# More column products by seven, folded norm factors, and values copied to blocks in DRAM: one encoder layer on one core

## The chip, the cores and the metric

The kernel runs on one core of a Trainium2 chip. Times are device microseconds. The time before is a median of 1103.4 us of three runs (1100.61 to 1104.03). The profile shows one further execution, with a span of 1101.0 us and a time of 1102.79 us. Engines are TensorE (PE, with its weight loads as PEld), VectorE (DVE), ScalarE (ACT), GpSimd (POOL) and SyncE (SP); SP issues nearly all DMAs, in order.

## The reference

One layer, 2048 tokens of width 1024, 16 heads of 64, all float32. The token grid is 32 rows by 64 columns.

```python
h = rmsnorm(x, g)                            # h = x * rsqrt(mean(x^2) + 1e-6) * g
q, k, v, gate = split(h @ w_in, 4)           # w_in is 1024 x 4096
# neighbourhood attention: a query at (row, col) sees 8 rows x 16 columns of keys,
# s = q.k / 8 + bias(head, row offset, col offset), softmax, o = p @ v
x = x + (o * silu(gate)) @ w_out
out = rmsnorm(x, norm_f)
```

## The kernel before, in words

Precision: every matrix operand is split into a high part rounded to fp32r and a low part, and each product is three matmuls, high by high, high by low and low by high. A matmul moves 512 columns.

The tokens are four column blocks c of 512, c = 0 to 3 (8 grid rows each). A *unit* is 256 output columns of q, k or the gate g; `(kind, j)` with j = 0 to 3 names them, and one unit holds two head pairs hp = 2j and 2j + 1. Values v are made in two units u, token tile t by token tile (t = 0 to 15).

**Stage one** (`stage_one`) makes v for tiles 0 to 7 and all 12 units of k, q, g for the token blocks 0 and 1. The units go by `seven_products`: the product of a 2 x 2 block matrix (two halves of the input width by two halves of the unit's columns, against two token blocks) is formed from seven block products in place of eight, in the order 1, 6, 2, 7, 5, 4, 3. One block product is 12 matmuls (4 k-tiles by 3), so a unit is 84. Its inputs are token blocks B11, B12, B21, B22 (first index: half of the input width, second: token block) and sums T1 to T4 of them, made once; and weight quarters A11 to A22 with sums S1 to S4, made for each unit on DVE (`sum_`). Each is split by `form` (ACT, then DVE), up to six products ahead. After the products, `keep`, `add` and `out_` combine the PSUM banks into the four outputs. `out_` adds on DVE and multiplies by `rb[c]` on GpSimd; `evac` does the fourth output with one DVE multiply. `rb[c]` is the reciprocal root mean square of the 512 tokens of block c, spread over the partitions: `diagonal(c)` puts it on four diagonal matrices, `spread_rstd(c)` multiplies by ones (two matmuls) and copies the bank (ACT). The gain g is put in when the x blocks are split (`split_to` with a scale). `give` then finishes an output: k into a high and a low part, g to g(1 + tanh(g/2)), q as it is; and it queues the store to DRAM (`k_hi`, `k_lo`, `sgd`, `qd`).

**Stage two** (`stage_two`) makes v for tiles 8 to 15 and the units of `units_two`, three of them (k, q, g with j = 0), by seven products for the token blocks 2 and 3. `evac_v` scales by the reciprocal root mean square of the token (`rt`).

**Attention** is a loop of 64 pairs, plus two to drain. A step is one head pair p and one row block T (8 query rows, up to 15 key rows); a *pair* is half of a step, two of the four column groups C. `order` has T = 0 for all p first, then T = 1 and 2, then T = 3. Iteration i does, in this order on each engine: `begin(i)` (mask additions `bias` on GpSimd, and loads asked for), `feed` (other TensorE work), `middle(i)` (split of the queries), `feed` again, `normalise(i-1)` (reciprocal on DVE, multiply on GpSimd), `turns(i-2)` (transposes of the probabilities, copied out of PSUM by DVE, L1011, and ACT, L1010), `scores(i)` (L963; mask and minimum on DVE, L970; exponential on ACT, L973), `values(i-2)` (L1031, and after a step's second pair the product with the gate, L1045).

`feed(n)` takes n matmuls from a generator, so that TensorE has work while the other engines do the softmax. Its second call has `calm` 8: it goes on, up to 12 matmuls, until 8 have passed since the last item given to DVE and ACT. `amount[i]` is 22 matmuls for the first 48 pairs and 19.7 for the last 18. The fill is first `projections`: the columns of k, q, g with j = 1 to 3 for token blocks 2 and 3, in `halves`, two groups of 24 matmuls each (`group`, lines L365, L367, L369), evacuated at once by `evac` (`pending`, `flush`). Then `outputs`: the output projection, tile by tile (L1223 to L1227), with `split_og` (L1103, L1104) of the loaded attention output, residual, and final norm. What is left of it runs alone after the loop.

Loads and stores are closures in the list `later` with a due time in matmuls of fill; `due` issues them on SP. `must` issues a store early if a load needs it. Tiles come from pools with a fixed number of buffers, each freed when its last reader is done; a DMA into a buffer still in use waits on SP, and with it all DMAs behind it. The value cache `vd` has the layout [head pair, grid row mod 4, column, row group, 128]; `load_v` (L920) reads a block for a column group by four DMAs, one for each row within a group of four. A program lists the functions that the diff touches:

## Time and profile before

| | |
|---|---|
| median of three runs | 1103.4 us (1100.61 to 1104.03) |
| profiled execution | 1102.79 us, span 1101.0 us |
| TensorE busy | 1080.7 us, 98% |
| DVE, ACT, POOL busy | 732.7, 531.5, 378.5 us |
| DMA traffic | 217.29 MB, mean 197 GB/s |
| granted TensorE clock, mean | 0.99 |

A row of the table of stretches is: start and end; duration; busy time of PE, PEld, DVE, ACT and POOL, each with its number of instructions; granted clock; busy share of the DMA engines; GB/s. A row of a group has busy time and mean ns of one, then the idle time of the engine before them with what ended it. In a timeline row the bracket is the idle time before the first instruction of the row and its releaser. In the chain of waits a row is start, length, and what ran.

### The profile page before, as it was taken

The numbers are of one execution on the slowest core, as the hardware profiler recorded it, in microseconds if no ns is written. First come the engines' busy times: TensorE is split into PE (matmuls) and PEld (weight loads), VectorE is DVE, ScalarE is ACT, GpSimd is POOL, SyncE is SP. The second block draws the span as 40 slices with busy tenths as digits, with TensorE's granted clock in tenths as the row PEclk, the third lists the DMA queues.
The fourth block names the chain that finished last, engine by engine and source line by source line (L and its number), as shares of the span: only waits on it lengthen the run. The fifth ranks groups of instructions, "written<-read, shape, count | busy, mean of one in ns | idle before, by whom it ended". The sixth has DMA issues, their size and how long they took to land.

```text
span 1101.0 us, 22543 instructions
## 1 busy us (share of the span) xinstructions
PE 1080.7 (98%) x7657; PEld 883.6 (80%) x7657; DVE 732.7 (67%) x1663; ACT 531.5 (48%) x1336; POOL 378.5 (34%) x483
## 2 busy tenths in 40 slices
PE   9999999999999999999999999999999999999997
PEld 6888888888888888877888888888877888887885
DVE  5376778788777337575665766665777777776644
ACT  7545343343344433255554554564556555555422
POOL 0000312222130001245445444424447666675200
PEclk9999999999999999998999999999999999999999
DMA  8633545454574235587767878687979797887452
GB/s 307 209 96 105 185 132 181 143 173 112 166 216 138 80 89 157 195 263 232 233 193 241 251 223 230 211 268 222 259 237 286 228 288 225 252 274 211 152 153 77
DMA packets 142962, 217.29 MB, mean 197 GB/s; under 512 B 18048, under 2 KB 65408, under 8 KB 142848
## 3 DMA queue, kind: packets, MB, share of 16 engines
q1 hardware_dynamic: 142704, 215.58, 64.6%
q8 instruction: 62, 1.02, 0.4%
q14 instruction: 52, 0.43, 0.1%
q10 hardware_dynamic: 144, 0.26, 0.1%
HBM read 157.05 MB, written 58.72 MB: 196 GB/s over the span
## 4 chain that ended last, share of the span: by engine, by line
PE 88%; DVE 5%; DMA 3%; issue 2%; ACT 1%; POOL 1%; SPq 0%; DVEq 0%; POOLq 0%
PE pp L421 24%; PE pv L534 16%; PE o L1031 7%; PE s L963 6%; PE pp L369 6%; PE pp L367 6%; PE pp L365 5%; PE po L1227 5%; PE po L1223 4%; PE po L1225 4%; PE ph L986 4%; ACT x L973 1%; PE zp L1242 1%; DVE gl L1104 1%; DMA sgt<-sgd 0%
## 5 line engine op out<-in xcount | busy, mean ns | idle before, releaser
L981 POOL TENSOR_SCALAR x<-x,st 128x360 f32<-128x360 f32 (+5 forms) x256 | 143.1, 579 | 239.1 <-DVE st L979 157.1
L439 POOL TENSOR_TENSOR tmp<-tmp,rb 128x512 f32<-128x512 f32 x45 | 73.5, 1634 | 399.2 <-DVE tmp L438 358.4
L973 ACT ACTIVATE x<-x,st 128x360 f32<-128x360 f32 (+5 forms) x256 | 151.8, 594 | 56.4 <-DVE st L970 56.4
L421 PE MATMUL pp<-h,f 128*128 128x512 f32 x480 | 155.4, 389 | 0.0
L945 POOL TENSOR_TENSOR em<-e,mk 128x480 f32<-128x480 f32 (+5 forms) x160 | 140.8, 915 | 5.0 <-DVE st L970 5.0
L421 PE MATMUL pp<-t,f 128*128 128x512 f32 x540 | 129.8, 389 | 0.1
L970 DVE CUSTOM_DVE_ANT_0 x<-s,em 128x360 f32<-128x360 f32 (+5 forms) x256 | 123.8, 538 | 5.1 <-PE s L963 2.0
L421 PEld LDWEIGHTS pp<-t,f 128*128 128x128 f32 x540 | 101.3, 188 | 21.5 <-DVE u L432 0.6
L369 PE MATMUL pp<-h,w 128*128 128x512 f32 x288 | 115.9, 403 | 0.0
L367 PE MATMUL pp<-l,w 128*128 128x512 f32 x288 | 114.2, 397 | 0.0
L365 PE MATMUL pp<-h,w 128*128 128x512 f32 x288 | 113.6, 394 | 0.0
L1010 ACT ACTIVATE pta<-ph 96x256 f32<-96x256 f32 (+1 forms) x224 | 58.8, 333 | 105.8 <-PE ph L986 105.8
L1031 PEld LDWEIGHTS o<-pta,vt 96*64 96x64 f32 (+2 forms) x1792 | 86.0, 139 | 24.2 <-DVE pta L1011 10.2
L421 PEld LDWEIGHTS pp<-h,f 128*128 128x128 f32 x480 | 90.1, 188 | 18.8
L1031 PE MATMUL o<-pta,vt 96*64 96x128 f32 (+4 forms) x1792 | 95.2, 258 | 7.5 <-DVE pta L1011 4.6
L1227 PE MATMUL po<-wol,gh 128*128 128x512 f32 x252 | 101.4, 403 | 0.0
L1223 PE MATMUL po<-woh,gh 128*128 128x512 f32 x252 | 100.0, 397 | 0.0
L1225 PE MATMUL po<-woh,gl 128*128 128x512 f32 x252 | 99.7, 395 | 0.0
L1011 DVE COPY pta<-ph 128x384 f32<-128x384 f32 (+3 forms) x128 | 60.5, 513 | 51.5 <-PE ph L986 51.2
L421 PE MATMUL pp<-l,f 128*128 128x512 f32 x240 | 93.4, 389 | 0.0
L534 PE MATMUL pv<-wh,h 128*128 128x512 f32 x256 | 88.1, 390 | 0.0
L534 PE MATMUL pv<-wh,l 128*128 128x512 f32 x256 | 88.0, 389 | 0.0
(136 smaller groups left out, 1951.1 us busy)
## 6 DMA issues: line engine op xcount, KB each, us to landing
raw<-in_wg_dram SPq DMA_DIRECT2D x126, 256.0 KB
e<-in_rpb_dram SPq DMA_DIRECT2D x54, 240.0 KB
vt<-vd SPq DMA_DIRECT2D x256, 48.0 KB
row<-in_xr_dram SPq DMA_DIRECT2D x32, 256.0 KB
vd<-v SPq DMA_DIRECT2D x32, 256.0 KB
k_hi<-hi SPq DMA_DIRECT2D x32, 256.0 KB
k_lo<-lo SPq DMA_DIRECT2D x32, 256.0 KB
qd<-tmp SPq DMA_DIRECT2D x32, 256.0 KB
```

The costliest lines, as they stand in the source:

```text
L365: nc.tensor.matmul(p, wh[w, b][:, cols], hh[k, c], start=(k == 0), stop=False)
L367: nc.tensor.matmul(p, wh[w, b][:, cols], hl[k, c], start=False, stop=False)
L369: nc.tensor.matmul(p, wl[w, b][:, cols], hh[k, c], start=False, stop=(k == NK - 1))
L421: nc.tensor.matmul(B[n, P], t[:, int(m == 2), c], x[k][int(m == 1)], start=P in (1, 6, 5) and k == 0 and m == 0, stop=k == 3 and m == 2, s ...
L534: nc.tensor.matmul(ps[t], a[:, o], b, start=k == 0 and m == 0, stop=k == NK - 1 and m == 2)
L945: (nc.gpsimd if attending[0] or not s else nc.vector).tensor_tensor(sh(t), E[p, s][:, u0 + 4:u1 + 4, v0 + 8:v1 + 8], sh(MK[0][:, m0:m0 + n ...
L973: nc.scalar.activation(X[i, C][s], X[i, C][s], AF.Exp, bias=st[:, s:s + 1], scale=-1.0, accum_out=st[:, 2 + s:3 + s])
L981: nc.gpsimd.tensor_scalar(X[i, C][s], X[i, C][s], st[:, 4 + s:5 + s], 0.5, op0=OP.mult, op1=OP.mult)
L1031: nc.tensor.matmul(o[s * 64:s * 64 + 64, C * 128 + q0:C * 128 + q0 + nq], vt[C][:k, g - g0_, s * 64:s * 64 + 64], t[:k, at:at + nq], start ...
L1223: nc.tensor.matmul(p, gh, woh[q, j], start=(i == 0), stop=False)
L1225: nc.tensor.matmul(p, gl, woh[q, j], start=False, stop=False)
L1227: nc.tensor.matmul(p, gh, wol[q, j], start=False, stop=(i == NK - 1))
```

## The change

Six units are made by seven products in stage two (j = 0 and 1) in place of three; `halves` keeps j = 2 and 3, and `amount` follows by its formula: 16 matmuls for each of the first 48 pairs.

For the token blocks 2 and 3 the gain and the reciprocal root mean square go into the input blocks: `normed` multiplies a block of x by both in place on DVE, before it is split or summed. The outputs of stage two and of `projections` are then not scaled: `give` reads the bank itself. `diagonal(2)`, `spread_rstd(2)` and `diagonal(3)` move into the last units of stage one, `spread_rstd(3)` to the first value tiles of stage two. The gate is no longer kept in the column-blocked order; the product with the attention output reorders it.

Values are copied from `vd` to `vc[p, C]`, one DRAM tile for each head pair and column group, in two halves of rows (`copy_v`): 32 copies in stage one's products (three to a unit), 32 in the last value tiles and the products of stage two. `load_v` then needs one DMA for a block.

Queries are loaded two steps ahead into a pool of one buffer (`lp`) and split one step ahead, in the second pair of a step. The due times of the loads of values, keys, bias rows and gate change. `quiet` is a flag that lets `split_og` go two turns ahead in the second pair of a step, and late otherwise.

```diff
+    vc = {(p, C): dram.tile([4 * (c1 - c0), 8, 128], F32, name=f"vc{p}_{C}")
+          for p in range(NP) for C, (c0, c1) in enumerate(KEY_COLS)}
...
         if kind == "x":
-            split_x(a, b, t, (hh[a, b], hl[a, b]))
+            normed("x%d1" % (a // 4 + 1), b, a % 4, t)
+            split_to(hh[a, b], hl[a, b], t, None)
...
-    units_two = [(k, j) for j in range(1) for k in "kqg"]
-    halves = [(k, j, 1, c) for j in range(1, 4) for g in (("k", "q", "g") if j < 3 else ("k", "qg")) for c in (2, 3) for k in g]
+    units_two = [(k, j) for j in range(2) for k in "kqg"]
+    halves = [(k, j, 1, c) for j in range(2, 4) for g in (("k", "q", "g") if j == 2 else ("k", "qg")) for c in (2, 3) for k in g]
...
-    def give(kind, hp, c, tmp):
+    def give(kind, hp, c, t, psum=False):
...
         if kind == "q":
-            store(("q", hp, c), 12, lambda: nc.sync.dma_start(qd[hp][:, s], tmp))
+            if psum:
+                o = ev([128, 512], F32, "q")
+                nc.scalar.activation(blocked(o), tiled(t), AF.Copy)
+                t = o
+            store(("q", hp, c), 12, lambda: nc.sync.dma_start(qd[hp][:, s], t))
...
-        nc.scalar.activation(v, p, AF.Copy, scale=rt[:, t:t + 1])
+        nc.scalar.activation(v, p, AF.Copy, scale=rt[:, t:t + 1] if t < 8 else 1.0)
...
             nc.vector.tensor_tensor(lay(tmp), of(B[n, P]), of(u), OP.add)
-            nc.gpsimd.tensor_tensor(lay(tmp), lay(tmp), of(rb[c]), OP.mult)
+            if c0 == 0:
+                nc.gpsimd.tensor_tensor(lay(tmp), lay(tmp), of(rb[c]), OP.mult)
...
+    def normed(f, c, k, t):
+        nc.vector.scalar_tensor_tensor(t, t, gain(f, k), rb[c], op0=OP.mult, op1=OP.mult)
...
+    def copies(h, n):
+        for _ in range(n):
+            if uncopied[h]:
+                copy_v(*uncopied[h].pop(0))
...
         def also(n, i):
             m = n + len(us) - 1
+            if m and i in (1, 3, 5):
+                copies(0, 1)
...
+            if (n, i) == (-3, 1):
+                diagonal(2)
+            if (n, i) == (-3, 3):
+                spread_rstd(2)
...
+        norms = {(-2, 3): ("x11", 0), (-2, 5): ("x11", 1), (-1, 0): ("x11", 2), (-1, 1): ("x11", 3),
+                 (-1, 3): ("x21", 0), (-1, 4): ("x21", 1), (-1, 5): ("x21", 2), (-1, 6): ("x21", 3)}
...
         def also(n, i):
+            copies(1, 1)
...
-        def rows(r):
-            if r == 0:
-                VT[p, T, C] = vp([128, 4, 128], F32, "vt")
-            nc.sync.dma_start(VT[p, T, C][r * w:r * w + w, :g1_ - g0_].rearrange("p g d -> p (g d)"), src[r])
-
-        return [lambda r=r: rows(r) for r in range(4)]
+        def block():
+            VT[p, T, C] = t = vp([128, 4, 128], F32, "vt")
+            nc.sync.dma_start(t[:4 * (c1 - c0), :g1_ - g0_], vc[p, C][:, g0_:g1_])
+
+        return [block]
+
+    def copy_v(p, C, h):
+        must(*[("v", p // 4, t) for t in range(8 * h, 8 * h + 8)])
+        c0, c1 = KEY_COLS[C]
+        g = slice(512 * h, 512 * h + 512)
+        nc.sync.dma_start(vc[p, C].rearrange("(r c) g d -> c r (g d)", r=4)[:, :, g],
+                          vd[p // 4][p % 4].rearrange("r c g d -> c r (g d)")[c0:c1, :, g])
...
-            nc.vector.tensor_tensor(og, o, SG.pop((p, T)), OP.mult)
+            nc.vector.tensor_tensor(blocked(og), blocked(o), tiled(SG.pop((p, T))), OP.mult)
...
-            if n < ready["loaded"] and place[n] <= k + 1 and clock[0] - loaded_at[n] >= 28 and whole(n):
+            near = 2 if quiet[0] else 1 if i >= 4 else 0
+            if n < ready["loaded"] and place[n] <= k + near and clock[0] - loaded_at[n] >= 28 and whole(n):
...
     def begin(i):
         all_loads()
         m = i // 2
+        if 0 < i <= N:
+            p, T, cs = pairs[i - 1]
+            later_loads(load_v(p, T, cs[0]) + load_v(p, T, cs[1]), 0, 2)
...
                 nx = order[m + 1]
-                LOADS[m + 1] = kh, _, kl = load_qk(*nx)
-                later_loads([kh, kl], 0, 2)
+                kh, kl = load_k(*nx)
                 if nx[0] != p:
-                    later_loads(load_e(nx[0]), 4, 2)
-        if 0 < i <= N:
-            p, T, cs = pairs[i - 1]
-            later_loads(load_v(p, T, cs[0]) + load_v(p, T, cs[1]), 1, 1.5)
+                    later_loads(load_e(nx[0]), 5, 3)
+                later_loads([kh, kl], 9, 4)
         if i % 2 == 0 and 2 <= i <= N:
             p, T = order[m - 1]
-            later_loads([lambda: load_sg(p, T)], 7, 0)
+            later_loads([lambda: load_sg(p, T)], 15, 0)
 
     def middle(i):
-        if i % 2 or i >= N:
-            return
         m = i // 2
-        if type(QT[order[m]]) is not tuple:
-            split_q(*order[m])
-        if m + 1 < len(order):
-            later_loads([LOADS[m + 1][1]], 1, 0)
+        if i % 2 and m + 1 < len(order):
+            split_q(*order[m + 1])
+        if i == 0 or i % 2 and m + 2 < len(order):
+            later_loads([load_q(*order[m + (2 if i else 1)])], 1, 0)
...
         begin(i)
-        feed(a * 0.45)
+        feed(a * 0.25)
+        quiet[0] = i % 2 == 1 or i >= N
+        feed(a * 0.2)
         middle(i)
         feed(a * 0.55, 8)
+        quiet[0] = i >= N
```

## The prediction

> **What bounds the kernel now.** First the page's head and its table of engines.

> ```profile
> span 1101.0 us, 22543 instructions
> PE 1080.7 (98%) x7657; PEld 883.6 (80%) x7657; DVE 732.7 (67%) x1663; ACT 531.5 (48%) x1336; POOL 378.5 (34%) x483
> ```

> TensorE is busy in all but 20.3 us, so the time is its work plus what interrupts it. The second view is the table of stretches, one row per stage: from 97.4 the seven-product units of stage one, from 316 mostly the value tiles of stage two, from 414.5 its seven-product units, from 471.3 attention in three parts.

> ```profile
> 97.40:316.00 218.60, 218.47 (x964) 180.60 (x963) 172.44 (x252) 82.18 (x158) 53.95 (x33) 1.00 0.51 155
> 316.00:414.50 98.50, 98.50 (x436) 81.50 (x435) 54.17 (x86) 44.52 (x75) 4.97 (x3) 1.00 0.46 127
> 414.50:471.30 56.80, 56.80 (x252) 47.02 (x252) 39.91 (x55) 18.74 (x33) 13.77 (x9) 1.00 0.55 180
> 471.30:621.00 149.70, 146.43 (x1262) 118.72 (x1261) 94.23 (x270) 78.27 (x240) 75.10 (x117) 0.98 0.77 234
> 621.00:820.00 199.00, 196.84 (x1971) 160.26 (x1970) 130.46 (x345) 108.12 (x317) 88.65 (x124) 0.99 0.81 239
> 820.00:1044.00 224.00, 218.73 (x2152) 179.21 (x2152) 161.76 (x480) 125.67 (x368) 135.61 (x187) 0.98 0.79 239
> ```

> After the duration each row has PE, PEld, DVE, ACT and POOL busy, then the granted clock, the DMA share and GB/s. The projection stages have no gap at all. Attention lacks 3.3 + 2.2 + 5.3 = 10.7 us of PE and shows a clock under 1.00. Third, stretches of 10 us and TensorE's timeline show that this sits in four places.

> ```profile
> 490.00:500.00 10.00, 7.02 (x58) 5.17 (x58) 7.61 (x24) 6.18 (x19) 9.20 (x14) 0.80 0.90 274
> 500.00:510.00 10.00, 10.00 (x90) 8.17 (x87) 4.70 (x17) 5.13 (x19) 6.54 (x11) 0.86 0.63 191
> ...
> 810.00:820.00 10.00, 8.18 (x54) 6.83 (x55) 7.78 (x19) 6.08 (x15) 3.03 (x5) 0.83 0.92 289
> ...
> 830.00:840.00 10.00, 8.22 (x68) 6.91 (x65) 7.75 (x18) 5.64 (x17) 4.50 (x6) 0.83 1.01 317
> ...
> 1010.00:1020.00 10.00, 9.12 (x69) 7.35 (x70) 3.81 (x12) 3.30 (x12) 5.92 (x9) 0.83 0.60 174
> ```

> ```profile
> 495.54 0.43 PE L963 MATMUL s<-kt,qh 64*128 64x352 f32 x1 [1.47 <-DVE tmp L326]
> 497.15 0.95 PE L963 MATMUL s<-kt,qh 64*128 64x352 f32 x3 [1.18 <-ACT pta L1010]
> ...
> 811.83 1.56 PE L1031 MATMUL o<-pta,vt 96*64 96x128 f32 x32 [2.04 <-DVE pta L1011]
> ...
> 833.30 2.34 PE L1031 MATMUL o<-pta,vt 96*64 96x128 f32 x32 [1.78 <-DVE pta L1011]
> ...
> 1010.88 0.92 PE L1031 MATMUL o<-pta,vt 96*64 96x128 f32 x12 [1.64 <-DMA vt<-vd]
> ```

> The waits add to 1.47 + 1.18 + 2.04 + 1.78 + 1.64 = 8.1 us. Each is followed by a slow clock: the five rows lack (0.20 + 0.14 + 0.17 + 0.17 + 0.17) x 10 = 8.5 us of full clock, of which some 0.6 fall into the wait itself (half clock during the 1.18). So the four events cost 8.1 + 7.9 = 16.0 us, 4.0 each.

> How long the clock stays down is in a row behind the shortest of these waits:

> ```profile
> 1012.00:1014.00 2.00, 2.00 (x5) 1.55 (x6) 1.21 (x2) 0.00 (x0) 1.80 (x2) 0.50 0.45 148
> ```

> A wait of 1.64 us was enough for half the clock. [...]

> **The change part by part: TensorE's work.** A unit by seven products is 84 matmuls, and the same columns as half-groups are 4 x 24 = 96.

> ```profile
> L421 PE MATMUL pp<-h,f 128*128 128x512 f32 x480 | 155.4, 389 | 0.0
> L421 PE MATMUL pp<-t,f 128*128 128x512 f32 x540 | 129.8, 389 | 0.1
> L421 PE MATMUL pp<-l,f 128*128 128x512 f32 x240 | 93.4, 389 | 0.0
> L365 PE MATMUL pp<-h,w 128*128 128x512 f32 x288 | 113.6, 394 | 0.0
> ...
> 97.56 70.73 PE pp L421 x312
> ```

> L421 runs 480 + 540 + 240 = 1260 = 15 units; the three lines of `group` run 3 x 288 = 864. Three units move: +252 and -288, net -36. One matmul takes 70.73 / 312 = 0.2267 us of the chain, so this is **-8.2 us**, certain as long as TensorE is the bound.

> **Stage two's new units.** Stage one's row gives DVE 172.44 / 218.6 = 79%, that is 15.0 of the 19.0 us of a unit (84 x 0.2267), without a gap in PE. Three more such units in stage two fit the same way, and easier: `out_` no longer sends tiles through GpSimd there, and the scaling after the product goes.

> ```profile
> L439 POOL TENSOR_TENSOR tmp<-tmp,rb 128x512 f32<-128x512 f32 x45 | 73.5, 1634 | 399.2 <-DVE tmp L438 358.4 <-DMA raw<-in_wg_dram 12.9 <-DMA qr<-qd 12.0
> L328 DVE TENSOR_TENSOR tmp<-pp,rb 128x512 f32<-128x512 f32 x34 | 23.4, 689 | 37.1 <-PE pp L369 31.2 <-PE pp L421 5.8
> L705 DVE SCALAR_TENSOR_TENSOR spot<-spot,g,land 128x512 f32<-128x512 f32 x3 | 2.1, 746 | 0.0
> ```

> In their place `normed` adds 16 block multiplies and 4 in the re-split of x, near 0.75 us each (the L705 row, same form): 20 x 0.75 = 15 us of DVE. Eight of them, 6 us, fall into the last two units before the end of stage one, whose DVE has 2 x 4.0 = 8 us free. I take zero; if queued forms come late the bound is about 6 us. `spread_rstd(2)` moves into stage one and keeps its two matmuls. `spread_rstd(3)` needs a third buffer's release: its ACT copy waits for the last GpSimd multiply (1.6 us) of stage one, and behind it stand weight splits of a stage with ACT at 45%: zero to 2 us, I take zero.

> **The copies.** 64 DRAM-to-DRAM copies of 192 or 256 KB, 14.3 MB read and written, are queued on SP in the product phases and the last value tiles. No row shows such a copy. Bounds: nothing, if they use idle DMA time (share 0.51 and 0.55, so about 0.45 of some 300 us free); at most, moving 28.7 MB at the 317 GB/s of the row above is 91 us of DMA, less than the 135 free. I take nothing. SP is in order, so a copy that waits for a value store delays weight loads behind it; these have two units of lead.

> **Attention.** Its value loads drop from four DMAs a block to one:

> ```profile
> L920 SPq DMA_DIRECT2D vt<-vd x512: 289/379/1847, 480.2 to 1035.9; - x171
> ```

> 512 x 0.38 = 194 us of SP become 128 x 0.38 = 49. This aims at the event at 1010, where a block row stood late in SP's queue. Queries are split one step ahead, which takes `split_q` out of the path of the event at 490. `quiet` keeps the split of attention output (ahead of the late copies at 811 and 833) mostly to pairs without mask additions. Evacuation loses 0.69 us of DVE per group of 24 matmuls (row L328).

> Against it: fill per pair (`amount`) falls from 22 to 16 matmuls in 48 pairs.

> ```profile
> 514.33 1.26 PE o L1031 x24
> 522.62 1.26 PE o L1031 x24
> ...
> 659.24 1.49 PE o L1031 x32
> 668.52 1.49 PE o L1031 x32
> ...
> 697.04 1.49 PE o L1031 x32
> 703.40 1.49 PE o L1031 x32
> ...
> 801.31 0.85 PE ph L986 x23
> 807.58 0.84 PE ph L986 x23
> ```

> A pair lasts 8.29 us in row block 0 and 9.28 in the middle ones; six matmuls less (1.36 us) make 6.9 and 7.9. The wait for calm already made shorter pairs: 6.36 us up to 703.40, without a gap, and 6.27 up to 807.58, with the event at 811 at its end. The chain that has to fit is scores, minimum, exponential, reciprocal:

> ```profile
> 728.35 0.70 PE L963 MATMUL s<-kt,qh 64*128 64x480 f32 x4
> ...
> 732.07 0.58 ACT L973 ACTIVATE x<-x,st 128x360 f32<-128x360 f32 x1
> ```

> From 728.35 to 732.65 it is 4.3 us; the copies of the next transposes stand behind the reciprocal on DVE, about 0.8 us before the next scores. At 7.9 us the slack is 7.9 - 0.8 - 4.3 = 2.8 us, before 4.2. A pair that calm shortens by another 6 matmuls has 1.4 left, and one DVE or ACT item of fill in the wrong place uses that up. No row prices how often; from none of 48 pairs to one in five, at 4.0 us each (a full event): 0 to 40 us. I take two events, 8 us: of the two pairs of 6.3 us shown, one passed and one did not, and few will be as short.

> **Sum** against the profiled execution, 1102.8 us (span 1101.0 and 1.8 around it, 0.6 under the median of 1103.4): 1102.8 - 8.2 - 16.0 + 8 = **1086.6, say 1086**.

> **Rivals.** (1) *The work alone*: old events go, equivalents take their places, or the old ones stay. 1102.8 - 8.2 = 1094.6. For it: the last 18 pairs keep their 19.7 matmuls, and two events lie there or in the outputs. 25%.

> (2) *All four gone, none new*: 1102.8 - 24.2 = 1078.6. For it: each is addressed by its own part; against: thinner cover. 17%.

> (3) *Slower: the copy of the transposes behind a late reciprocal* in short pairs. PE then waits at the value matmuls, the clock halves, 4.0 us a time. It decides from (1106.7 - 1078.6) / 4.0 = 7 events; ten, one in five of the 48 pairs, give 1118.6. For it: exactly this wait (L1031 on L1011) made two of the four events, one of them behind the pair of 6.27 us. Against: DVE's share does not rise. It is 130.46 / 199 = 66% of 9.28 us, 6.1 us; fill's part drops by about 0.9 (less fill, no evacuation), 5.2 of 7.9 us. 12%.

> (4) *No change: transfers late*.

> ```profile
> raw<-in_wg_dram SPq DMA_DIRECT2D x126, 256.0 KB
> k_hi<-hi SPq DMA_DIRECT2D x32, 256.0 KB
> ```

> A pair of 9.28 us at 239 GB/s moves 2.2 MB. Fill's part, per 24 matmuls one weight load and on average 341 KB of stores, is 0.55 MB and becomes 0.40; 2.07 MB in 7.9 us is 261 GB/s, and the share goes from 0.81 to about 0.88. Stretches at 0.9 to 1.0 stand at the events above. Six such lateness events give 1102.6. Against: loads are asked for earlier, and SP is freed. 8%.

> **How the numbers follow.** Forecast 38%, (1) 25, (2) 17, (3) 12, (4) 8. The first three are faster by more than 0.3% (3.3 us, what can be told from no change here): 0.80; (4) is the same, 0.08; (3) slower, 0.12. The range leaves out case (3) and a little below (2), where the DVE and clock have nothing more to give: 1075 to 1103.

> **What would show it.** TensorE's matmul records must be 1512 at the seven-product line and 576 in `group`. The stretch from the end of stage one to the first scores must grow by 252 x 0.2267 = 57 us with PE still full, or the DVE and copy terms are wrong. Pairs must be 6.9 and 7.9 us apart. The 10 us rows must show at most two dips of the clock in attention; seven mean (3), and a releaser "DMA" on PE in most of them means (4). The time is wrong if attention's PE gaps do not shrink from 10.7 us.

## The result and the profile after

The changed kernel takes 1089.77 us (median of 4 runs, 1089.14 to 1090.56), against 1103.72 us of the kernel before beside it. The ratio is 0.9876, 95% interval 0.985 to 0.9902. The forecast was 1086, the range 1075 to 1103. The profiled execution took 1089.2 us.

The head of the changed kernel's page:

```profile
span 1087.3 us, 21925 instructions
PE 1067.7 (98%) x7621; PEld 872.2 (80%) x7621; DVE 729.0 (67%) x1680; ACT 535.1 (49%) x1354; POOL 357.3 (33%) x474
```

The next view has the matmuls by line: count, duration in ns (smallest, median, largest), first and last start. First two rows of the kernel before (L421 the seven-product line, L1031 the values), then the changed kernel: L411 is the seven-product line, L355 one of the three of `group`, L1056 the values.

```profile
L421 PE MATMUL pp<-h,f x480: 388/389/389, 97.4 to 471.2; 128*128 128x512 f32 x160
...
L1031 PE MATMUL o<-pta,vt x1792: 219/272/476, 498.5 to 1044.2; 96*64 96x128 f32 x56, 128*64 128x128 f32 x55, 96*64 96x64 f32 x44, 128*64 128x64 f32 x25
```

```profile
L411 PE MATMUL pp<-t,f x648: 387/389/499, 98.6 to 524.6; 128*128 128x512 f32 x162
...
L411 PE MATMUL pp<-h,f x576: 388/389/398, 95.9 to 527.4; 128*128 128x512 f32 x192
...
L411 PE MATMUL pp<-l,f x288: 389/389/389, 96.1 to 527.1; 128*128 128x512 f32 x144
...
L355 PE MATMUL pp<-h,w x192: 387/389/632, 527.6 to 785.2; 128*128 128x512 f32 x192
...
L1056 PE MATMUL o<-pta,vt x1792: 219/272/421, 550.3 to 1030.4; 96*64 96x128 f32 x56, 128*64 128x128 f32 x55, 96*64 96x64 f32 x44, 128*64 128x64 f32 x25
```

L411 has 648 + 576 + 288 = 1512 matmuls, and `group` 3 x 192 = 576. Attention runs from 527.6 to 1030.4, 502.8 us, where it took 572.8 us before (471.4 to 1044.2). The tail behind it is 56.9 us in both. The 36 matmuls fewer are there, and stage two is longer by 57.7 us, where 57 were forecast, once the start of the seven-product units (1.5 us earlier in this execution) is taken off.

The table of stretches of the changed kernel, cut at the stages and at the places where gaps lie:

```profile
97.40:316.00 218.60, 218.25 (x962) 180.03 (x961) 181.09 (x269) 82.96 (x160) 54.04 (x33) 1.00 0.61 190
...
413.30:527.60 114.30, 114.30 (x506) 94.65 (x506) 68.17 (x108) 36.66 (x65) 3.29 (x4) 1.00 0.62 193
527.60:560.00 32.40, 28.53 (x209) 22.08 (x208) 22.45 (x64) 19.17 (x56) 14.69 (x23) 0.95 0.81 258
560.00:786.00 226.00, 226.00 (x2448) 184.87 (x2448) 142.83 (x444) 141.60 (x436) 119.91 (x187) 1.00 0.86 266
786.00:872.00 86.00, 81.71 (x909) 64.68 (x909) 68.06 (x186) 53.52 (x161) 58.08 (x77) 1.00 0.84 262
872.00:1030.40 158.40, 156.79 (x1540) 128.33 (x1538) 110.86 (x348) 89.00 (x263) 96.07 (x139) 1.00 0.75 238
```

The products of stage two have no gap, as forecast. From 560 to 786 us, some 30 pairs with 16 matmuls of projections as fill, TensorE has no gap either: thin cover alone costs nothing there. The gaps are at two other places: 3.9 us in the first pairs, with a slow clock, and 4.3 us from 786 to 872, where the fill turns from projections to the output projection (the last matmul of L355 starts at 785.2). With 1.6 us later this makes 9.8 us, where attention lacked 10.7 before. So the gaps as such hardly shrank. The clock gained more: attention has 3.4 us at half clock, where it had 17.1, by the traces' records of the granted clock. TensorE's waits in the changed kernel, first pairs and then 700 to 900 us (total, times, longest; L988 the scores, L995 their mask, L1035 and L1036 the copies of the transposes, L342 the low part of a key output, L1252 and L1129 the output projection and its split):

```profile
PE s L988 <- ACT pta L1035: 1.6, 1, 1.6
PE s L988 <- DVE st L995: 1.3, 1, 1.3
PE s L988 <- DVE lo L342: 0.8, 1, 0.8
...
PE s L988 <- ACT pta L1035: 1.6, 4, 0.6
PE o L1056 <- DVE pta L1036: 1.3, 1, 1.3
PE po L1252 <- DVE gl L1129: 0.7, 1, 0.7
```

No wait of TensorE on a DMA is left. An event here is a wait of TensorE with the slow clock behind it, and cover is the fill that keeps TensorE busy meanwhile. Three of the four old events have no successor; in the first pairs there is still one. What came new are waits under 1.4 us, with the clock at 1.00 in the rows from 560 us on.

### The profile page after: what moved, and what is told of

It reads as the page before. It is cut to its first block, busy times and chain, and to the rows that moved or that the text cites. A ratio compares the mean times of both kernels' runs of the same rounds, so it can differ in the third digit from the quotient of the medians.

```text
span 1087.3 us, 21925 instructions
## 1 busy us (share of the span) xinstructions
PE 1067.7 (98%) x7621; PEld 872.2 (80%) x7621; DVE 729.0 (67%) x1680; ACT 535.1 (49%) x1354; POOL 357.3 (33%) x474
## 4 chain that ended last, share of the span: by engine, by line
PE 90%; DVE 5%; ACT 2%; issue 1%; DMA 1%; SPq 0%; POOL 0%; DVEq 0%; ACTq 0%; POOLq 0%
PE pp L411 28%; PE pv L531 16%; PE o L1056 8%; PE s L988 6%; PE po L1254 5%; PE po L1252 5%; PE po L1250 5%; PE ph L1011 4%; PE pp L359 4%; PE pp L357 4%; PE pp L355 4%; ACT x L998 1%; DVE f L394 1%; PE zp L1269 1%; DMA spot<-in_xt_dram 1%
## 5 line engine op out<-in xcount | busy, mean ns | idle before, releaser
L970 POOL TENSOR_TENSOR em<-e,mk 128x480 f32<-128x480 f32 (+5 forms) x160 | 136.1, 888 | 191.7 <-DVE u L422 189.8
L411 PE MATMUL pp<-h,f 128*128 128x512 f32 x576 | 186.5, 389 | 0.0
L411 PE MATMUL pp<-t,f 128*128 128x512 f32 x648 | 155.9, 389 | 0.4 <-DVE u L422 0.2
L430 POOL TENSOR_TENSOR tmp<-tmp,rb 128x512 f32<-128x512 f32 x36 | 58.9, 1637 | 269.9 <-DVE tmp L428 243.7
L411 PEld LDWEIGHTS pp<-t,f 128*128 128x128 f32 x648 | 121.5, 188 | 26.4 <-DVE u L422 1.2
L995 DVE CUSTOM_DVE_ANT_0 x<-s,em 128x360 f32<-128x360 f32 (+5 forms) x256 | 123.9, 539 | 4.9 <-POOL x L1006 1.5
L411 PEld LDWEIGHTS pp<-h,f 128*128 128x128 f32 x576 | 108.1, 188 | 22.4
L411 PE MATMUL pp<-l,f 128*128 128x512 f32 x288 | 112.0, 389 | 0.0
L1035 ACT ACTIVATE pta<-ph 96x256 f32<-96x256 f32 (+1 forms) x224 | 58.5, 332 | 95.7 <-PE ph L1011 95.6
L1252 PE MATMUL po<-woh,gl 128*128 128x512 f32 x252 | 99.2, 394 | 0.7 <-DVE gl L1129 0.7
L1056 PEld LDWEIGHTS o<-pta,vt 96*64 96x64 f32 (+2 forms) x1792 | 84.0, 137 | 18.1 <-issue 9.3
L1036 DVE COPY pta<-ph 128x384 f32<-128x384 f32 (+3 forms) x128 | 60.5, 513 | 56.0 <-PE ph L1011 55.5
L1056 PE MATMUL o<-pta,vt 96*64 96x128 f32 (+4 forms) x1792 | 92.8, 255 | 2.3 <-DVE pta L1036 2.0
L531 PE MATMUL pv<-wl,h 128*128 128x512 f32 x256 | 87.9, 389 | 0.0
L988 PE MATMUL s<-kt,qh 64*128 64x480 f32 (+5 forms) x512 | 81.5, 365 | 6.5 <-ACT pta L1035 3.6
L394 DVE TENSOR_TENSOR f<-raw,f 128x512 fp32r<-128x512 f32 x90 | 69.2, 769 | 21.2 <-ACT f L393 21.2
## 6 DMA issues: line engine op xcount, KB each, us to landing
raw<-in_wg_dram SPq DMA_DIRECT2D x126, 256.0 KB, 4.9
row<-in_xr_dram SPq DMA_DIRECT2D x32, 256.0 KB, 4.3
vd<-v SPq DMA_DIRECT2D x32, 256.0 KB, 3.0
k_hi<-hi SPq DMA_DIRECT2D x32, 256.0 KB, 2.6
k_lo<-lo SPq DMA_DIRECT2D x32, 256.0 KB, 4.3
vc<-vd SPq DMA_DIRECT2D x32, 256.0 KB, 4.9
```

The lines of the kernel that those rows point to most:

```text
L394: nc.vector.tensor_tensor(t[:, 1], src, t[:, 0].bitcast(F32), OP.subtract)
L411: nc.tensor.matmul(B[n, P], t[:, int(m == 2), c], x[k][int(m == 1)], start=P in (1, 6, 5) and k == 0 and m == 0, stop=k == 3 and m == 2, s ...
L531: nc.tensor.matmul(ps[t], a[:, o], b, start=k == 0 and m == 0, stop=k == NK - 1 and m == 2)
L970: (nc.gpsimd if attending[0] or not s else nc.vector).tensor_tensor(sh(t), E[p, s][:, u0 + 4:u1 + 4, v0 + 8:v1 + 8], sh(MK[0][:, m0:m0 + n ...
L988: nc.tensor.matmul(pst[s], qq[a, qs], kk[a, :r1 - r0, c0:c1], start=(m == 0), stop=(m == 2))
L995: nc.vector.tensor_tensor_reduce(X[i, C][s], pst[s], EM[p, ROW_TYPE[T], COL_TYPE[C], s], -1.0, 1e38, OP.add, OP.min, st[:, s:s + 1])
```

## The experiments

All ratios are to the kernel before, timed beside each run. Its own median beside them was 1101.4 us (for three_rows, queries_one_step, no_quiet and pool_and_later) or 1103.6 to 1103.8, so kernels of different groups are compared by their ratios.

| kernel | median us | ratio | 95% interval |
|---|---|---|---|
| the change | 1089.8 | 0.9876 | 0.985 to 0.9902 |
| three_units | 1086.0 | 0.9838 | 0.982 to 0.9856 |
| value_rows | 1125.1 | 1.0189 | 1.0158 to 1.022 |
| three_rows | 1101.5 | 0.9998 | 0.9985 to 1.0011 |
| three_rows_copies | 1099.5 | 0.9963 | 0.9948 to 0.9977 |
| queries_one_step | 1100.1 | 0.998 | 0.9961 to 0.9998 |
| no_quiet | 1089.5 | 0.989 | 0.9871 to 0.9908 |
| resplit_pool | 1088.0 | 0.9858 | 0.9843 to 0.9873 |
| fill_later | 1083.5 | 0.9819 | 0.9802 to 0.9836 |
| pool_and_later | 1080.3 | 0.9806 | 0.9788 to 0.9824 |
| query_due_later | 1084.7 | 0.9831 | 0.9812 to 0.9849 |
| start_cover | 1080.2 | 0.9794 | 0.9775 to 0.9813 |
| three_pool_later | 1085.5 | 0.9839 | 0.982 to 0.9858 |

**The units by seven products undone: three_units.**

```diff
-    units_two = [(k, j) for j in range(2) for k in "kqg"]
-    halves = [(k, j, 1, c) for j in range(2, 4) for g in (("k", "q", "g") if j == 2 else ("k", "qg")) for c in (2, 3) for k in g]
+    units_two = [(k, j) for j in range(1) for k in "kqg"]
+    halves = [(k, j, 1, c) for j in range(1, 4) for g in (("k", "q", "g") if j < 3 else ("k", "qg")) for c in (2, 3) for k in g]
```

> The changed kernel with three units by seven products in stage two again, so 22 matmuls of fill for each of the first 48 pairs; all other parts stay changed. Work theory (the units are worth their 36 matmuls, 36 x 0.2267 = 8.2 us, and the thinner fill costs nothing): 1089.8 + 8.2 = 1098.0 us. Rival, thin cover (16 matmuls let gaps through, 4.3 us of TensorE idle time in the stretch from 786 to 872 us where fill turns to the output projection): with 22 these go, and the time is 1098.0 - 4.3 = about 1093.7 us. If the gaps stay with 22 they belong to the output projection's own DVE and ACT work.

It is faster than the changed kernel, by 3.7 us (the two intervals just overlap), with 36 matmuls more. This goes further than the rival: the thin fill takes 8.2 + 3.7 = about 12 us. Its stretches (start, projections, change to the outputs, rest):

```profile
471.80:505.00 33.20, 32.01 (x236) 25.60 (x235) 22.90 (x65) 21.48 (x60) 13.98 (x22) 1.00 0.83 267
505.00:805.00 300.00, 299.91 (x2978) 246.26 (x2977) 170.08 (x511) 167.61 (x504) 143.56 (x215) 1.00 0.79 245
805.00:891.00 86.00, 85.55 (x861) 69.16 (x860) 64.95 (x184) 54.55 (x159) 52.32 (x70) 1.00 0.86 269
891.00:1027.70 136.70, 135.44 (x1314) 110.94 (x1313) 94.10 (x301) 74.61 (x219) 79.36 (x118) 1.00 0.74 230
```

Attention takes 555.9 us here, 53.1 more than in the changed kernel, where 288 matmuls more would be 65.3: 12.2 us are lost with 16. The gaps add to 3.0 us against 9.8, which explains 6.8, and the clock of the first pairs (0.95 over 32.4 us) 1.6. The first pairs take 4.3 us of this: 1.2 us of gap at full clock with 22 matmuls, 3.9 us and the slow clock with 16. The other 3.8 us stand in no idle row. A matmul's record is 0.389 us long and the next starts after 0.227, so a wait under 0.16 us cannot be seen; that this is where they are is only argued.

**The value loads: value_rows, three_rows, three_rows_copies.** The first reads values by four DMAs a block from the old layout and makes no copies; the due times of the value loads go back with them, so the two are not separated; the second does this with three units; the third is the second with the 64 copies made and not read.

```diff
-            nc.sync.dma_start(t[:4 * (c1 - c0), :g1_ - g0_], vc[p, C][:, g0_:g1_])
+            nc.sync.dma_start(VT[p, T, C][r * w:r * w + w, :g1_ - g0_].rearrange("p g d -> p (g d)"), src[r])
...
-            later_loads(load_v(p, T, cs[0]) + load_v(p, T, cs[1]), 0, 2)
+            later_loads(load_v(p, T, cs[0]) + load_v(p, T, cs[1]), 1, 1.5)
```

> The changed kernel without the copies in DRAM: values are read by four DMAs a block from the old layout, at the old due times. Theory that one DMA a block removed the waits for late transfers: a wait of TensorE on a value load (1.6 us and half a clock, 4.0 us as before) comes back once to three times, since the fill is thinner and SP issues 384 DMAs more in a shorter attention: 1094 to 1102 us. Rival, the copies only moved the traffic and the other parts removed the waits: 1089.8 within 2 us, or less by what the 28.7 MB of copies cost.

> Three units by seven products in stage two (22 matmuls of fill) and values read by rows without the copies in DRAM: the difference to three_units (1086.0) is the worth of the copies with full cover, as 1125.1 - 1089.8 = 35.3 us is it with 16. Theory: by rows the kernel before showed one wait on a value load, 4.0 us with its clock, so 1088 to 1092 us, and most of the 35 us come from the thinner fill and the loads together. Rival, the loads by rows cost the same whatever the fill (SP issues 384 DMAs more): 1086 + 35 = 1121 us.

> three_rows (1101.5 us) with the 64 copies in DRAM made as in the changed kernel, but not read: the value loads still take four DMAs a block. It prices the copies alone. Theory of the prediction, they lie in idle DMA time of stages whose TensorE has no gap: 1101.5 within 2 us. Rival, their traffic or SP's waits in front of them delay weight loads: a gap appears in the seven-product stages and the time is 1104 us or more.

Neither theory had the size. One DMA a block, with its due times, is worth 3.1% (35 us) with 16 matmuls of fill and 1.6% (15 to 18 us) with 22. With three units and rows, nothing is left of the gain: 0.9998; so the folded norm factors, the earlier queries and `quiet`, which three_rows keeps, gain nothing together without the single loads. The copies themselves cost nothing: 1099.5 us with them (0.9963), 1101.5 without (0.9998). They even stand 0.35% lower, with intervals that do not touch; why, no run shows.

The traces have the loss as gaps and slow clock. Attention of value_rows has 31.7 us of gaps and 30.7 us at half clock (9.8 and 3.4 in the changed kernel), which makes 35.6 of the 37.3 us that it takes longer. Attention of three_rows, in the next rows, has 12.2 us of gaps and 6.8 at half clock (3.0 and none in three_units), 12.7 of 13.9 us:

```profile
471.80:505.00 33.20, 29.52 (x219) 23.36 (x220) 22.92 (x65) 20.55 (x58) 13.90 (x22) 1.00 0.72 221
...
895.00:1041.40 146.40, 139.98 (x1344) 114.24 (x1339) 96.03 (x307) 75.65 (x223) 79.76 (x119) 0.99 0.78 228
```

TensorE's longest waits in value_rows, and below them waits of SP on transfers of other buffers in the kernel before, in three_rows and in the changed kernel (L920, L943, L938 are the value loads):

```profile
PE o L1061 <- DMA vt<-vd: 12.1, 6, 3.3
PE o L1061 <- ACT qh L495: 2.9, 1, 2.9
PE o L1061 <- DMA sgt<-sgd: 2.7, 1, 2.7
```

```profile
SPq L920 <- DMA kt<-k_lo: 8.1, 10, 1.1
SPq L920 <- DMA e<-in_rpb_dram: 8.0, 15, 0.9
```

```profile
SPq L943 <- DMA kt<-k_lo: 16.6, 21, 1.6
SPq L943 <- DMA kt<-k_hi: 14.9, 18, 1.5
SPq L943 <- DMA ograw<-ogd: 9.9, 9, 2.2
```

```profile
SPq L938 <- DMA sgt<-sgd: 1.1, 2, 0.7
```

Summed over all such rows, SP waited for earlier DMAs 195 times, 109 us, in the kernel before, 190 times, 118 us, in three_rows, and 68 times, 31 us, in the changed kernel. These waits come on top of the time to issue, which stays the larger part: 512 x 0.38 = 194 us for the value loads before, 128 x 0.32 = 41 us after (0.32 us is their median there).

**Queries one step ahead again: queries_one_step.** In `middle` the queries of a step are split in its own first pair, and the next are loaded behind.

```diff
-        if i % 2 and m + 1 < len(order):
-            split_q(*order[m + 1])
+        if type(QT[order[m]]) is not tuple:
+            split_q(*order[m])
```

> The changed kernel with queries loaded one step ahead and split in the first pair of their own step, as before the change. Theory of the prediction: the early split took the queries out of the path of the first pairs' event, so it grows again, and with the thin fill waits on the split queries appear elsewhere: 1092 to 1098 us. Rival: it changes nothing outside the first pairs, which still have their event for another reason: 1089.8 within 1.5 us.

By the ratios it is 1.0% slower than the changed kernel, beyond the slow end of the theory. The first pairs have a small part in it: 0.5 us of gap more, and 6.8 us at half clock in place of 3.4 (no_quiet has 6.8 there too). The rest of the 8.8 us that attention takes longer is spread, with 4.7 us of gaps more in all and a slow stretch at 884 us, as the waits of TensorE show (L496 is the split of the queries):

```profile
PE s L988 <- DVE ql L496: 3.6, 6, 1.0
PE o L1056 <- DVE pta L1036: 3.1, 2, 1.9
```

**Without quiet: no_quiet.**

```diff
-            near = 2 if quiet[0] else 1 if i >= 4 else 0
+            near = 1
```

> The changed kernel where the split of the attention output may again come one turn ahead in any pair. Theory: in pairs with mask additions on GpSimd the split holds up the copies of the transposes, two events of 4 us as at 811 and 833 before: 1094 to 1099 us. Rival: the due time of this split matters little, since the fill of 16 already has gaps in the same stretch: 1089.8 within 1.5 us.

The rival holds: 1089.5 us, and by the ratios (0.989 against 0.9876) the same within the intervals.

**The two places of the gaps: resplit_pool, fill_later, pool_and_later.**

The first hunk is resplit_pool, the second fill_later; pool_and_later has both.

```diff
-            normed("x%d1" % (a // 4 + 1), b, a % 4, t)
-            split_to(hh[a, b], hl[a, b], t, None)
+            nc.gpsimd.tensor_tensor(t, t, rb[b], OP.mult)
+            split_to(hh[a, b], hl[a, b], t, g0[:, a:a + 1])
...
-    amount = [early / 48] * 48 + [(384 - 30) / 18] * 18
+    amount = [14.5] * 36 + [(early - 522) / 12] * 12 + [(384 - 30) / 18] * 18
```

> The changed kernel with one edit: in the four re-splits of x at the end of stage two the multiply by the norm row goes to GpSimd and the gain into the split, so DVE has one instruction of 0.8 us in place of two of 0.7 with a wait for ACT between. Theory: DVE's queue of re-splits from 526 to 537 us holds up the mask of the first scores, and that is the one event left (3.9 us of idle TensorE from 530 to 550 and 1.7 us of clock): it shrinks by most of this, 1085 to 1087 us. Rival, the backlog is that of the weight splits and key outputs, or of transfers (DMA share 1.0 from 532 to 538): 1089.8 within 1 us, the gap stays.

> The changed kernel with the same 768 matmuls of fill over the first 48 pairs, spread as 14.5 for 36 pairs and 20.5 for 12, in place of 16 each. Theory: a pair filled with projections needs less than 16 (from 640 to 786 us TensorE has no gap), a pair filled with the output projection needs more; the gaps from 786 to 872 us (4.3 us) fall under 2 us and no others come: 1086 to 1088 us. Rival, 16 is near the edge in the early pairs already: at 14.5 gaps appear there and the time is 1091 us or more. Third: the gaps come from single DVE items of the output projection whatever the fill: 1089.8 within 1 us.

> Both edits that gained alone: the re-split of x on GpSimd (1088.0 against 1089.8 us) and the fill of 14.5 and 20.5 matmuls (1083.5). If the two act in different places, the first pairs and the change to the output projection, the gains add: 1089.8 - 1.8 - 6.3 = 1081.7 us. Rival: at 14.5 the first pairs have too little cover, so that the event at the start moves to another instruction, and the time stays at 1083.5 within 1 us.

The first gains 1.8 us, between its theory and its rival, with intervals that overlap the changed kernel's. In the changed kernel's chain of waits the re-splits are seen one after the other: DVE multiplies, ACT copies, DVE subtracts, and the next multiply waits behind.

```profile
533.62 0.67 DVE raw L488
...
534.37 0.64 ACT h L492
...
535.04 0.69 DVE l L493
535.73 0.67 DVE raw L488
...
536.49 0.64 ACT h L492
```

The second gains 6.3 us, more than its theory. Its stretches for the projections and for the change to the outputs:

```profile
560.00:797.00 237.00, 236.94 (x2648) 194.12 (x2647) 152.75 (x480) 152.78 (x473) 135.97 (x208) 1.00 0.88 272
797.00:883.00 86.00, 85.75 (x887) 69.77 (x886) 65.86 (x182) 54.73 (x160) 56.04 (x73) 1.00 0.86 273
```

The gaps at the change of fill fall from 4.29 to 0.25 us, and 14.5 matmuls of projections still cover a pair from 560 us on. With both edits the time is 1080.3 us. The forecast for added gains was 1081.7. By its ratio, 0.9806, the time would be 1082.3 us beside a kernel before of 1103.7, 0.13% under fill_later alone, with intervals that overlap. And the event at the start moved to another instruction (the scores wait 2.3 us for L342), as the rival had it. So the times fit the sum, but do not rule the rival out.

**What is left at the start: query_due_later, start_cover.** Both start from pool_and_later. The first asks for the queries later, the second gives the first four pairs more fill.

```diff
-            later_loads([load_q(*order[m + (2 if i else 1)])], 1, 0)
+            later_loads([load_q(*order[m + (2 if i else 1)])], 6, 0)
```

```diff
-    amount = [14.5] * 36 + [(early - 522) / 12] * 12 + [(384 - 30) / 18] * 18
+    amount = [20] * 4 + [13.8] * 32 + [(early - 521.6) / 12] * 12 + [(384 - 30) / 18] * 18
```

> pool_and_later (1080.3 us) with the query load due 6 matmuls after the split in place of 1. Its trace has one event left, at 547 us: SP stood at the query load, whose one buffer the late split frees, and behind it a weight load came late, the weight split on DVE, and a bank of the scores (2.3 us of wait and half a clock). Theory: SP no longer waits there, the weight load is 3 to 4 us earlier, and the event goes: 1076 to 1078 us. Rival: the backlog is that of DVE, and SP's place in it changes nothing: 1080.3 within 1 us.

> pool_and_later with 20 matmuls of fill in the first 4 pairs, 13.8 in the next 32 and 20.5 in 12. Theory that the event at the start is one of cover: with 5.5 matmuls more (1.2 us) a pair it shrinks or goes, 1076 to 1079 us, if 13.8 is still enough for the pairs behind. Rival, the items of fill themselves make the backlog, so more of them per pair do not help: 1080 to 1083 us.

The first theory fell: slower by 4.4 us in the medians and 2.8 by the ratios. The wait on the key output is still there, a new one has come beside it, and the half clock lasts 10.2 us in place of 3.4.

```profile
PE ph L1011 <- POOL x L1006: 2.3, 3, 1.9
PE s L988 <- DVE lo L342: 2.1, 1, 2.1
```

With more cover the first pairs lose little and keep the clock, yet the time is the same within the intervals, 1080.2 us:

```profile
527.50:560.00 32.50, 31.51 (x233) 25.12 (x232) 25.23 (x66) 19.70 (x56) 18.11 (x26) 1.00 0.90 269
```

What took this gain back is not settled.

**Six units against three, both with cover: three_pool_later** (the two edits on three units, 20.5 and 26.5 matmuls).

> Three units in stage two with the same two edits (re-split on GpSimd, fill 20.5 for 36 pairs and 26.5 for 12). It prices the six units when neither version lacks cover. Theory: the 36 matmuls are then worth their 8.2 us, and this is 1080.3 + 8.2 = 1088.5 us less what it has fewer in gaps; three_units has 1086.0 without the edits, so at most that: 1083 to 1086 us, which leaves the six units 3 to 6 us. Rival, six units are worth nothing even then: 1080.3 within 1.5 us.

1085.5 us, against 1080.3 for pool_and_later and 1080.2 for start_cover: placed well, the six units bring 3.6 us (by the ratios to pool_and_later) to 5.3 us (against start_cover, timed beside it) of the 8.2.

## Why the prediction was right, and where it was not

The range and the direction held, and of the cases the forecast is the nearest, 3.8 us off, with the work alone (1094.6) 4.8 us off on the other side. The sum had three terms, and the runs price each. Three_units has the old number of matmuls and all other parts, and is 1.62% faster than before, 17.9 us.

| term | forecast | measured |
|---|---|---|
| 36 matmuls fewer | -8.2 | -8.2 by counts and lengths |
| the four old events | -16.0 | -17.9 (three_units) |
| events of thin cover | +8 | +12 (the change less three_units, plus 8.2) |

**Work of TensorE.** Right, and stage two takes it without a gap: DVE's room was read rightly from stage one's row.

**The old events.** The size was right: attention of three_units is 16.8 us shorter than before, with 7.7 us fewer in gaps and 17.1 us less at half clock, worth 8.5. The shares were not right, and that the total came out in spite of this is in part luck. I gave the value loads one event, 4.0 us; one DMA a block, with its due times, is worth 15 to 35 us. What failed is the step that priced a DMA by its issue time (512 x 0.38 us of SP) and by the single wait of TensorE that named it. The trace had the rest, which the sum left out: SP's own waits for unrelated transfers. Without the single loads the other parts bring nothing with three units (0.9998). That `quiet` removed the events at 811 and 833 is not borne out, since without it the time is the same; what did remove them was not separated.

**The queries.** They were to take the event at 490 away. With 22 matmuls of fill the first pairs do lose only 1.2 us, at full clock (three_units), though by which part was not separated. With 16 an event is back there, 3.9 us of gap and a slow clock. The early split gains 1.0%, most of it elsewhere.

**Thin cover.** I took two full events where one mechanism was short pairs, the copy of the transposes behind the reciprocal. From 560 us on the pairs with projections never showed it, down to 14.5 matmuls. My slack was figured from the length of a pair and did not ask what the fill holds: the output projection brings more DVE items per matmul than the projections. In the changed kernel's trace the lines of the fill have 39 DVE items with 506 matmuls from 560 to 786 us, and 41 with 134 matmuls from 797 to 872. That 16 was too little there and in the first pairs, and enough between, is shown by three_units, fill_later and start_cover; that the items are the reason is argued from these counts. So the mis-sized term is +8, measured 12: 4.3 us of gaps at the change of fill, 3.9 us with 1.6 us of clock at the start, 1.6 us of gaps later, less the 3.0 us of gaps that three_units has too, and 3.8 us that no idle row shows.

**Four re-splits of x.** I costed them as DVE time in a stage with room, at nothing. They fall just ahead of the first scores, in a queue where each waits for ACT: that is a part of the event there (1.8 us alone, 1.4 us by the ratios beside the other edit, neither clear of the intervals). Three_units has the same four re-splits there and loses only 1.2 us at full clock, so they make an event only where cover is thin.

**The copies.** Nothing, as taken (three_rows_copies).

**The rivals.** Transfers were not late: no wait of TensorE on a DMA, at 266 GB/s and a share of 0.86 where I had 261 and 0.88. The work alone (1094.6) had the right idea that something equal returns, but only 12 of the 17.9 did. The slower case needed seven events, and the clock dipped once in attention.

**Pair lengths.** 6.9 us in row block 0 was right; 7.9 in the middle blocks was not. The changed kernel's chain, for each:

```profile
584.66 1.26 PE o L1056 x24
591.53 1.26 PE o L1056 x24
...
661.63 1.49 PE o L1056 x32
...
758.27 1.49 PE o L1056 x32
```

The first two are 6.87 us apart; from 661.63, 13 pairs in 96.64 us are 7.43 us. I had read the old length off one pair (9.28 us), and calm makes neighbours differ by several matmuls.

## What to carry to other kernels

Cover is not a number of matmuls per step: count the items on the other engines that the covering work brings with it, and move cover to where it brings most; here the same 768 matmuls, spread otherwise, gained 6.3 us. Price a DMA on an in-order queue by the queue's own waits as well as by its issue time: four small loads for one cost 15 to 35 us, with TensorE naming DMAs for a part of it. And an edit that costs nothing on average is to be placed in time: four short instructions ahead of the first dependent step were a part of the one event in the first pairs.

## What the runs showed of the hardware that was not expected

SP, at a load of values, often waits until an earlier DMA, mostly to another buffer, has landed, by the releaser that the profile names: 52 us in 96 waits before, 69 us in 108 in three_rows, 3 us in 8 after. Over all lines it is 109 us in 195 waits before and 31 us in 68 after. The instruction records in the traces of these two kernels, before and after, show what the program asks for: SP's DMAs name eight completion semaphores in strict turn (1183 DMAs before, 863 after), and for 1173 and 848 of them SP has a wait on the semaphore that the DMA names, at its issue or just ahead of it. 192 of the 195 waits before and 62 of the 68 after end with an update of that semaphore, which the DMA issued eight before named last. A block read by four DMAs takes half of such a turn, a block read by one an eighth.

The clock does not follow from the length of a wait alone. Timeline rows of value_rows and of three_rows, each with the stretch that shows the clock behind it:

```profile
650.33 0.77 PE L1061 MATMUL o<-pta,vt 96*64 96x128 f32 x12 [1.43 <-ACT x L1003]
...
652.00:653.00 1.00, 1.00 (x4) 0.72 (x4) 0.69 (x2) 0.00 (x0) 1.00 (x2) 0.50 0.54 144
```

```profile
826.84 0.89 PE L1061 MATMUL o<-pta,vt 128*64 128x128 f32 x16 [1.45 <-ACT x L1003]
...
820.00:830.00 10.00, 8.55 (x88) 6.94 (x89) 6.55 (x19) 7.66 (x23) 7.39 (x10) 1.00 0.98 325
```

Of the other runs, value_rows shows half clock from 651.46 us (by rows of 1 us), with the 1.43 us inside the 3.41 us ahead of it. In no_quiet two waits of 0.51 and 0.70 us lie inside the 3.41 us ahead of half clock from 866.82. So 1.21 us in sum was followed by half clock there, and 1.30 us in the changed kernel was not.

The 4.3 us of short waits from 786 to 872 us in the changed kernel, 1.30 us at most in one piece, left the clock at 1.00. The single waits of 1.64, 1.78 and 2.04 us in the kernel before were each followed by 3.41 us at half clock, a loss of 1.7 us beside their own length. What decides for sums between 1.2 and 1.6 us, and what else it depends on, these traces do not show.
